# The down-projection of a SwiGLU layer by seven block products in place of eight

## The chip, the cores and the metric

One core of a Trainium2 chip runs the whole program. The metric is device microseconds of one execution; the kernel before took 1401.01 us, the median of 3 runs (1399.54 to 1403.0).

## The reference, cut to what matters

The program is a two-layer trunk over 512 rows of 1024 features (an attention mixer, a layer norm, a SwiGLU, a layer norm, a gated embedding, in each layer). The change touches the SwiGLU alone:

```python
def swiglu(x, w1, w3, w2):
    return (jax.nn.silu(x @ w1) * (x @ w3)) @ w2
...
x = layer_norm(DEEPNORM_ALPHA * x + swiglu(x, ffn_w1[i], ffn_w3[i], ffn_w2[i]), ln2_g[i], ln2_b[i])
```

The inner width is 2816, that is 22 tiles of 128 (the row tiles of w2). All data are float32. Each product is done in three TensorE passes on a high part rounded to fp32r and the remainder (high by low, high by high, low by high), which the helper `mm3` issues (L153 to L156).

## The kernel before

The rows of x lie in four SBUF tiles of 128 rows (`x[0]` to `x[3]`); their transposes, split into high and low parts, are `xTh` and `xTl`. `swiglu` walks over the 22 inner tiles in pairs. `up(f)` loads tile f of w1 and w3 in 512-column chunks of 256 KB through `wload` (L137: three `raw` buffers, a cast on ScalarE to the high part, a subtraction on VectorE or GpSimd, two to one, for the low part; four `hi` and four `lo` buffers of 128x1024). It makes two PSUM blocks of 24 matmuls each, then silu, the product of the two (L670), and the split of the result into high and low parts (`split`, L123 to L127), which are stationary operands of the down-projection.

`down(f0, gs)` loads two row tiles of w2 through the same `wload` and gives, for each of 4 row blocks and 2 column halves, 6 matmuls into one of two PSUM banks (`ps_pq`); VectorE adds each block to `x[t]` (L208 for the first pair, L212 after). So four inner tiles cost 16 PSUM blocks of 6, that is 96 matmuls. `down` of a pair is written after `up` of the next pair, and the last pair is done in `finish_rows` (L274), which adds the last blocks with their row sums and runs the layer norm of a row tile as soon as its two halves are there, then the transposes (`ps_xt`) and the first half of the gate (`ps_g`).

The order on each engine is not the written one: a scheduler orders the instructions ahead of time by written order as priority, by readiness of operands and by free buffers, with its own estimate of durations. On the chip each engine then runs its list in order. The pools that the change touches: `qk` (three buffers of 128x2048), `pl` (four of 128x1024), `pr` (two of 128x1536), `tmp` (four of 128x512), `g` (three of 128x2x512), `v` (eight of 128x1024), PSUM `ps_at` (4 banks), `ps_o` (2), `ps_pq` (2).

Of the kernel before, what the change touches and what calls it, by code (L numbers as in the profile page):

```python
# [8 lines left out]
F32 = mybir.dt.float32  # L9
F32R = mybir.dt.float32r  # L10
AF = mybir.ActivationFunctionType
ALU = mybir.AluOpType
AX = mybir.AxisListType

P = 128
LINE = 32
S = 512
NT = S // P
D = 1024
KT = D // P  # L20
DEPTH = 2
ALPHA = (2.0 * DEPTH) ** 0.25
# [18 lines left out]
QOFF = [0, 128, 384, 768]  # L41
WIDE = 1536
AHEAD = 0


@with_exitstack
def trunk(ctx: ExitStack, tc: tile.TileContext, a, out):
    nc = tc.nc

    def pool(name, bufs, **kw):  # L50
        return ctx.enter_context(tc.tile_pool(name=name, bufs=bufs, **kw))

    const = pool("const", 1)
    wpool = pool("w", 4)
    act = pool("act", 1)
# [3 lines left out]
    acts, dve, gps = nc.scalar, nc.vector, nc.gpsimd  # L59


    def temp(name, dtype=F32):
        return act.tile([P, S], dtype, tag="tmp", bufs=4, name=name)

    def wide(name, dtype=F32):
        return act.tile([P, WIDE], dtype, tag="pr", bufs=2, name=name)

    def spare(name, dtype=F32):
        return act.tile([P, D], dtype, tag="pl", bufs=4, name=name)

    def quad(name, dtype=F32R):
        return act.tile([P, 4, S], dtype, tag="qk", bufs=3, name=name)

    def row_tile(name, dtype=F32):
        return act.tile([P, D], dtype, tag="v", bufs=8, name=name)
# [4 lines left out]
    def bank(tag, bufs):  # L80
        return lambda name: psum.tile([P, S], F32, tag=tag, bufs=bufs, name=name)

    ps_at, ps_o, ps_pq = bank("at", 4), bank("o", 2), bank("pq", 2)
# [33 lines left out]

    xTh = const.tile([P, KT, S], F32R, name="xTh")
    xTl = const.tile([P, KT, S], F32R, name="xTl")
    x = [const.tile([P, D], F32, name=f"x{t}") for t in range(NT)]  # L120


    def split(hi, lo, src, scale=1.0, eng=None):  # L123

        if isinstance(scale, float) and scale == 1.0:
            nc.scalar.copy(hi, src)
            (eng or nc.vector).tensor_tensor(lo, src, hi.bitcast(F32), ALU.subtract)  # L127
        else:
            nc.scalar.mul(hi, src, scale)
            nc.vector.scalar_tensor_tensor(lo, src, scale, hi.bitcast(F32), ALU.mult, ALU.subtract)  # L130
# [8 lines left out]
    def wload(src, n, m):  # L139

        hi = wpool.tile([P, D], F32R, tag="hi", name="whi")
        lo = wpool.tile([P, D], F32R, tag="lo", name="wlo")
        for c in range(0, n * m, S):
            end = min(c + S, n * m)
            raw = wpool.tile([P, S], F32, tag="raw", bufs=3, name="wraw")[:, 0:end - c]
            nc.sync.dma_start(raw, src[:, c:end])
            count[0] += 1
            eng_hi, eng_lo = (v[count[0] % len(v)] for v in engines[0])
            (eng_hi.copy if eng_hi is acts else eng_hi.tensor_copy)(hi[:, c:end], raw)  # L149
            eng_lo.tensor_tensor(lo[:, c:end], raw, hi[:, c:end].bitcast(F32), ALU.subtract)  # L150
        return [t[:, 0:n * m].rearrange("p (n m) -> p n m", n=n) for t in (hi, lo)]

    def mm3(o, lhs, rhs, first, last):  # L153
        nc.tensor.matmul(o, lhsT=lhs[0], rhs=rhs[1], start=first, stop=False)  # L154
        nc.tensor.matmul(o, lhsT=lhs[0], rhs=rhs[0], start=False, stop=False)  # L155
        nc.tensor.matmul(o, lhsT=lhs[1], rhs=rhs[0], start=False, stop=last)  # L156

    def both(t, f):
        return (f(t[0]), f(t[1]))

    def row_piece(w, k):
        return wload(w[k * P:(k + 1) * P, :], 1, D)
# [3 lines left out]
    def blk(t):  # L166
        return slice(t * P, (t + 1) * P)
# [37 lines left out]
    def accumulate(t, half, ps, first, total=None):  # L205
        xs = x[t][:, half * S:(half + 1) * S]
        if first:
            nc.vector.scalar_tensor_tensor(xs, xs, ALPHA, ps, ALU.mult, ALU.add)  # L208
        elif total is not None:
            nc.vector.scalar_tensor_tensor(xs, xs, 1.0, ps, ALU.mult, ALU.add, accum_out=total)  # L210
        else:
            nc.vector.tensor_tensor(xs, xs, ps, ALU.add)  # L212

    def row_weights(w, rows):

        pieces = [row_piece(w, r) for r in rows]
        return lambda i, half: both(pieces[i], lambda v: v[:, 0, half * S:(half + 1) * S])

    def project_block(t, lhs, w, first, ps_of, sums=(None, None), halves=(0, 1)):

        n = len(lhs)
        for half in halves:
            ps = ps_of("ps_y")
            for i in range(n):
                mm3(ps, both(lhs[i], lambda v: v[:, blk(t)]), w(i, half), i == 0, i == n - 1)
            accumulate(t, half, ps, first, sums[half])
            yield 640 * n
# [32 lines left out]
    class Fill:  # L260
# [5 lines left out]
        def add(self, name, gen, after=()):  # L266
            self.items.append((name, gen, set(after)))

        def step(self):
            ready = [n for n, (_, _, after) in enumerate(self.items) if after <= self.done]  # L270
            if not ready:
                return None
            for n in ready[:1 + AHEAD]:
                name, gen, after = self.items[n]  # L274
# [350 lines left out]
    def gate(i, e, w, done):  # L625
        bg = broadcast(spare("bgate"), a["ple_b_gate"][i])
        pieces = [wload(w[0, c], 2, S) for c in range(4)]

        def block(t, half, cuts=1):
            ps = ps_at("ps_g")  # L630
            n = S // cuts
            for c in range(cuts):
                cs = slice(c * n, (c + 1) * n)
                hs = slice(half * S + c * n, half * S + (c + 1) * n)
                for k in range(KT):
                    mm3(ps[:, cs], x_block(k, t), both(pieces[k // 2], lambda v: v[:, k % 2, cs]), k == 0, k == KT - 1)
                s = temp("sg")[:, cs]
                nc.vector.tensor_tensor(s, ps[:, cs], bg[:, hs], ALU.add)
                nc.scalar.activation(s, s, AF.Sigmoid)
                nc.vector.tensor_tensor(s, s, e[t][:, hs], ALU.mult)  # L640
                nc.vector.tensor_tensor(x[t][:, hs], x[t][:, hs], s, ALU.add)
                if i == DEPTH - 1:
                    nc.sync.dma_start(out[0, blk(t), hs], x[t][:, hs])
            done(t, half)

        def rest():
            pieces[:] = [wload(w[1, c], 2, S) for c in range(4)]
            for t in range(NT):
                block(t, 1, 2 if i == DEPTH - 1 and t == NT - 1 else 1)

        return lambda t: block(t, 0), rest


    def swiglu(i, finish):
        w1, w3, w2 = a["ffn_w1"][i], a["ffn_w3"][i], a["ffn_w2"][i]
        nf = DFF // P

        def up(f, g, cuts=1):
            pieces = [wload(w[f], KT, P) for w in (w1, w3)]
            hps = [ps_at("ps_h") for _ in pieces]  # L660
            n = S // cuts
            for c in range(cuts):
                cs = slice(c * n, (c + 1) * n)
                for piece, ps in zip(pieces, hps):
                    for k in range(KT):
                        mm3(ps[:, cs], both(piece, lambda v: v[:, k, :]), both(xT, lambda v: v[:, k, cs]),
                            k == 0, k == KT - 1)
            s = temp("silu")
            nc.scalar.activation(s, hps[0], AF.Silu)
            nc.vector.tensor_tensor(s, s, hps[1], ALU.mult)  # L670
            split(g[0], g[1], s)

        def down(f0, gs):
            w = row_weights(w2, [f0 + j for j in range(len(gs))])
            for t in range(NT):
                for _ in project_block(t, gs, w, f0 == 0, ps_pq):
                    pass

        waiting = None
        for f in range(0, nf, 2):  # L680
            group = quad("gT")
            gs = [(group[:, 2 * j, :], group[:, 2 * j + 1, :]) for j in range(2)]
            for j in range(2):
                up(f + j, gs[j], 2 if f + j == 0 else 1)
            if waiting is not None:
                down(*waiting)
            waiting = (f, gs)
        f0, gs = waiting
        finish(gs, row_weights(w2, [f0 + j for j in range(len(gs))]))


    def mixer_mla_sb(norm, e):
# [293 lines left out]
    for i in range(DEPTH):  # L986
        def norm_params(gname, bname):
            return [broadcast(spare(n), a[n][i]) for n in (gname, bname)]
# [11 lines left out]
        def finish(gs, w):  # L1000
            first_half, rest = gate(i, e, a["w_gate"][i], done)
            finish_rows(gs, w, False, norm_params("ln2_g", "ln2_b"), after=first_half)
            rest()
# [105 lines left out]
```

## Time and profile before

| | |
|---|---|
| median of 3 runs | 1401.01 us (1399.54 to 1403.0) |
| profiled execution | 1401.66 us, span 1400.0 us |
| TensorE matmuls | 97% of the span busy |
| VectorE / ScalarE / GpSimd | 57% / 44% / 29% busy |
| mean granted TensorE clock | 0.993 of full speed |

The span is 40 slices of 35 us. The two SwiGLUs lie at about 303 to 652 us and at 985 to 1345 us. A busy TensorE is counted with modelled ends, so the distance between starts of matmuls says more than their durations. A VectorE instruction of the page overlaps the next one a little; the distance between starts is what it occupies.

### The profile page before, as it was taken

Reading aid. Unit: us, or ns where it says so; the run is one execution under the profiler, and the core shown is the slowest. Engines: PE = TensorE matmul, PEld = TensorE weight load, DVE = VectorE, ACT = ScalarE, POOL = GpSimd, SP = SyncE. Lnnn points to the kernel's source line nnn. Section 1 sums busy time; section 2 is a strip of 40 time slices with the busy share of each in tenths; the row PEclk is TensorE's granted clock in tenths of the full one; section 3 lists DMA queues with packets and bytes.
Section 4 is the critical chain, followed back from the end, with each engine's and each line's share of the span. In section 5 each row is a group of like instructions: output and inputs, shape, how many; then the busy total and the mean of one; then the engine's idle time right before and its main releaser. Section 6 shows DMA issues by size and latency. Waiting matters only on the chain.

```text
span 1400.0 us, 18875 instructions
## 1 busy us (share of the span) xinstructions
PE 1361.1 (97%) x6776; PEld 1139.6 (81%) x6776; DVE 797.0 (57%) x1492; ACT 611.6 (44%) x1269; POOL 408.8 (29%) x406
## 2 busy tenths in 40 slices
PE   8999999799999999999989999998999999999998
PEld 7888787588888888887879888876888888888877
DVE  4656778843444444448655775797434434444495
ACT  4656767552223222324456665754422223232252
POOL 5654733221111111112135454442211111111130
PEclk9999999999999999999999999999999999999999
DMA  6211312232322323332134222121423232322212
GB/s 232 94 40 42 125 60 73 78 117 80 106 91 91 105 94 107 102 102 78 62 107 137 91 91 69 64 88 68 136 76 104 94 105 100 110 91 98 98 61 98
DMA packets 69166, 131.75 MB, mean 94 GB/s; under 512 B 8128, under 2 KB 8896, under 8 KB 69056
## 3 DMA queue, kind: packets, MB, share of 16 engines
q1 hardware_dynamic: 66304, 120.75, 25.7%
q0 software_dynamic: 2768, 9.80, 2.1%
q8 instruction: 53, 0.87, 0.3%
q14 instruction: 41, 0.34, 0.1%
HBM read 127.80 MB, written 2.72 MB: 93 GB/s over the span
## 4 chain that ended last, share of the span: by engine, by line
PE 85%; DVE 7%; ACT 3%; DMA 3%; issue 2%; POOL 1%; SPq 0%; DVEq 0%; POOLq 0%; ACTq 0%
PE ps_h L154 11%; PE ps_h L155 11%; PE ps_h L156 11%; PE ps_y L154 7%; PE ps_y L155 7%; PE ps_y L156 7%; PE ps_qkT L154 2%; PE ps_qkT L155 2%; PE ps_qkT L156 2%; PE ps_o L408 2%; PE ps_g L154 2%; PE ps_g L156 2%; PE ps_g L155 2%; PE ps_z L545 1%; PE ps_t L440 1%
## 5 line engine op out<-in xcount | busy, mean ns | idle before, releaser
L150 POOL TENSOR_TENSOR wlo<-wraw,whi 128x512 fp32r<-128x512 f32 (+2 forms) x212 | 276.8, 1313 | 752.5 <-ACT whi L149 624.9
L149 ACT CAST whi<-wraw 128x512 fp32r<-128x512 f32 (+1 forms) x402 | 238.2, 616 | 553.8 <-PE ps_h L155 230.4
L154 PE MATMUL ps_h<-xTl,whi 128*128 128x512 f32 (+1 forms) x736 | 279.7, 380 | 0.0
L155 PE MATMUL ps_h<-xTh,whi 128*128 128x512 f32 (+1 forms) x736 | 279.5, 380 | 0.0
L156 PE MATMUL ps_h<-xTh,wlo 128*128 128x512 f32 (+1 forms) x736 | 279.3, 380 | 0.0
L150 DVE TENSOR_TENSOR wlo<-wraw,whi 128x512 fp32r<-128x512 f32 (+1 forms) x215 | 172.6, 816 | 133.3 <-ACT whi L149 132.4
L212 DVE TENSOR_TENSOR x<-x,ps_y 128x512 f32<-128x512 f32 x176 | 119.7, 682 | 145.8 <-PE ps_y L156 145.6
L156 PEld LDWEIGHTS ps_h<-xTh,wlo 128*128 128x128 f32 x736 | 138.2, 188 | 26.5
L155 PEld LDWEIGHTS ps_h<-xTh,whi 128*128 128x128 f32 x736 | 138.3, 188 | 26.3
L154 PEld LDWEIGHTS ps_h<-xTl,whi 128*128 128x128 f32 x736 | 138.4, 188 | 26.2
L155 PE MATMUL ps_y<-whi,gT 128*128 128x512 f32 x352 | 136.9, 389 | 0.0
L154 PE MATMUL ps_y<-wlo,gT 128*128 128x512 f32 x352 | 136.6, 390 | 0.0
L156 PE MATMUL ps_y<-whi,gT 128*128 128x512 f32 x352 | 136.1, 389 | 0.0
L670 DVE TENSOR_TENSOR silu<-silu,ps_h 128x512 f32<-128x512 f32 x44 | 30.3, 688 | 110.3 <-PE ps_h L156 108.4
L154 PE MATMUL ps_qkT<-xTl,whi 128*128 128x512 f32 x192 | 77.7, 405 | 1.7 <-ACT whi L149 0.9
L155 PEld LDWEIGHTS ps_y<-whi,gT 128*128 128x128 f32 x352 | 66.1, 188 | 13.7
L156 PEld LDWEIGHTS ps_y<-whi,gT 128*128 128x128 f32 x352 | 66.1, 188 | 13.7
L156 PE MATMUL ps_qkT<-xTh,wlo 128*128 128x512 f32 x192 | 77.2, 402 | 0.0
L154 PEld LDWEIGHTS ps_y<-wlo,gT 128*128 128x128 f32 x352 | 66.0, 188 | 13.6
L155 PE MATMUL ps_qkT<-xTh,whi 128*128 128x512 f32 x192 | 76.5, 399 | 0.0
L154 PE MATMUL ps_v<-wlo,xTh 128*128 128x256 f32 (+1 forms) x192 | 56.4, 294 | 6.6 <-DVE neg_tri L112 6.3
L155 PE MATMUL ps_v<-whi,xTh 128*128 128x256 f32 (+1 forms) x192 | 55.7, 291 | 0.0
(234 smaller groups left out, 2534.5 us busy)
## 6 DMA issues: line engine op xcount, KB each, us to landing
wraw<-in_ffn_w_dram SPq DMA_DIRECT2D x264, 256.0 KB, 2.7
wraw<-in_w_gate_dram SPq DMA_DIRECT2D x32, 256.0 KB, 2.8
wraw<-in_w_qkf_dram SPq DMA_DIRECT2D x32, 256.0 KB, 2.6
wraw<-in_w_qkb_dram SPq DMA_DIRECT2D x16, 256.0 KB, 2.8
wraw<-in_a_w_out_dram SPq DMA_DIRECT2D x16, 256.0 KB, 2.6
kbias<-nd_dram POOLq DMA_DIRECT2D x8, 512.0 KB, 5.0
wraw<-in_c_w_out_dram SPq DMA_DIRECT2D x16, 256.0 KB, 2.7
wraw<-in_w_vf_dram SPq DMA_DIRECT2D x15, 256.0 KB, 3.1
```

Source lines behind the costliest of these rows:

```text
L149: (eng_hi.copy if eng_hi is acts else eng_hi.tensor_copy)(hi[:, c:end], raw)
L150: eng_lo.tensor_tensor(lo[:, c:end], raw, hi[:, c:end].bitcast(F32), ALU.subtract)
L154: nc.tensor.matmul(o, lhsT=lhs[0], rhs=rhs[1], start=first, stop=False)
L155: nc.tensor.matmul(o, lhsT=lhs[0], rhs=rhs[0], start=False, stop=False)
L156: nc.tensor.matmul(o, lhsT=lhs[1], rhs=rhs[0], start=False, stop=last)
L212: nc.vector.tensor_tensor(xs, xs, ps, ALU.add)
L408: nc.tensor.matmul(o_ps[:, kb * P:], lhsT=val[:, c:c + 2 * HD], rhs=t, start=first and n == 0, stop=last and n == 1, skip_group_check=True)
L440: nc.tensor.transpose(u.ps[:, blk(qb - u.i)], u.h.pr[:, QOFF[qb] + u.i * P:QOFF[qb] + (u.i + 1) * P], ident)
L545: nc.tensor.matmul(u.z[:, c:u.n], lhsT=w, rhs=rhs, start=False, stop=i == len(mms) - 1, skip_group_check=True)
L670: nc.vector.tensor_tensor(s, s, hps[1], ALU.mult)
```

## The change

The inner tiles 0 to 19 are taken in five groups of four (the last pair, 20 and 21, stays as it was). The group's product, 512 rows by 512 inner columns by 1024 outputs, is cut in two along each dimension, and seven products of 256 x 256 x 512 are made from sums and differences of blocks in place of eight; each is 2 PSUM blocks of 6 matmuls (`ps_m`, in `ps_pq` and `ps_o`). The four inner tiles of a group are kept unsplit in float32 (`gb`, as blocks); the four row tiles of w2 come as two transfers of 1 MB into `w2raw`. `operands(m)` makes the sums of product m and splits both operands; it is written one product ahead. `down` is now a generator with one step for a product, and two steps are written behind each `up`; the last group's seven steps stand together, behind `up(20)`. Products 0, 5 and 6 are added to x at once, products 1 to 4 to running sums (`acc`, four tiles), which `flush()` adds to x, once in a layer, written between the last step and `up(21)`. `up(21)` stands directly ahead of `finish`.

```diff
--- before.py
+++ after.py
@@ -41,6 +41,7 @@
 QOFF = [0, 128, 384, 768]
 WIDE = 1536
 AHEAD = 0
+HALF = S // 2
 @with_exitstack
@@ -117,7 +118,8 @@
     xTh = const.tile([P, KT, S], F32R, name="xTh")
     xTl = const.tile([P, KT, S], F32R, name="xTl")
-    x = [const.tile([P, D], F32, name=f"x{t}") for t in range(NT)]
+    x_rows = const.tile([P, NT, D], F32, name="x")
+    x = [x_rows[:, t, :] for t in range(NT)]
     def split(hi, lo, src, scale=1.0, eng=None):
@@ -667,26 +669,137 @@
                             k == 0, k == KT - 1)
             s = temp("silu")
             nc.scalar.activation(s, hps[0], AF.Silu)
-            nc.vector.tensor_tensor(s, s, hps[1], ALU.mult)
-            split(g[0], g[1], s)
-        def down(f0, gs):
-            w = row_weights(w2, [f0 + j for j in range(len(gs))])
-            for t in range(NT):
-                for _ in project_block(t, gs, w, f0 == 0, ps_pq):
+            g(s, hps[1])
+        def as_parts(g):
+            def put(s, h):
+                nc.vector.tensor_tensor(s, s, h, ALU.mult)
+                split(g[0], g[1], s)
+            return put
+        def as_block(halves, p, k):
+            def put(s, h):
+                for n, half in enumerate(halves):
+                    fs = slice(n * HALF, (n + 1) * HALF)
+                    nc.vector.tensor_tensor(half[:, p, k, :], s[:, fs], h[:, fs], ALU.mult)
+            return put
+        sums = {}
+        def down(f0, halves):
+            first = f0 == 0
+            raw = []
+            for p in range(2):
+                t = quad("w2raw", F32)
+                nc.sync.dma_start(t.rearrange("p (k j) c -> p k (j c)", k=2),
+                                  w2[(f0 + 2 * p) * P:(f0 + 2 * p + 2) * P, :].rearrange("(k p) c -> p k c", k=2))
+                raw.append(t)
+            B = [[halves[i][:, :, k, :] for i in range(2)] for k in range(2)]
+            def W(j, k):
+                return [t[:, 2 * k + j, :] for t in raw]
+            s3, s1 = ([wide(n)[:, q * S:(q + 1) * S] for q in range(2)] for n in ("s3", "s1"))
+            n1, n2, n3, n4 = (temp(n).rearrange("p (q s) -> p q s", q=2) for n in ("n1", "n2", "n3", "n4"))
+            def add(o, a, b, eng):
+                for q in range(2):
+                    eng[q].tensor_tensor(o[q], a[q], b[q], ALU.add)
+            def operands(m):
+                tt = dve.tensor_tensor
+                ws, bs = [(W(0, 1), B[1][0]), (W(0, 0), B[0][0]), (s3, n3), (s1, n1), (s1, n2), (W(1, 1), n4),
+                          (s1, B[1][1])][m]
+                if m == 2:
+                    add(s3, W(0, 0), W(1, 0), (dve, gps))
+                    tt(n3, B[0][1], B[1][1], ALU.subtract)
+                elif m == 3:
+                    add(s1, W(1, 0), W(1, 1), (dve, gps))
+                    tt(n1, B[0][0], B[0][1], ALU.subtract)
+                elif m == 4:
+                    add(s1, s1, W(0, 0), (dve, gps))
+                    dve.scalar_tensor_tensor(n2, B[1][1], -1.0, n1, ALU.mult, ALU.subtract)
+                elif m == 5:
+                    tt(n4, n2, B[1][0], ALU.add)
+                elif m == 6:
+                    add(s1, s1, W(0, 1), (dve, gps))
+                parts = act.tile([P, 2, S], F32R, tag="g", bufs=3, name="bparts")
+                bh, bl = (parts[:, c, :].rearrange("p (q s) -> p q s", q=2) for c in range(2))
+                acts.copy(bh, bs)
+                dve.tensor_tensor(bl, bs, bh.bitcast(F32), ALU.subtract)
+                hi = wpool.tile([P, D], F32R, tag="hi", name="whi")
+                lo = wpool.tile([P, D], F32R, tag="lo", name="wlo")
+                wh, wl = ([v[:, q * S:(q + 1) * S] for q in range(2)] for v in (hi, lo))
+                for q in range(2):
+                    acts.copy(wh[q], ws[q])
+                    (dve, gps)[(q + m) % 2].tensor_tensor(wl[q], ws[q], wh[q].bitcast(F32), ALU.subtract)
+                return (bh, bl), (wh, wl)
+            ready = operands(0)
+            for m in range(7):
+                (bs, ws), ready = ready, operands(m + 1) if m < 6 else None
+                for tb in range(2):
+                    ps = (ps_pq, ps_o)[tb]("ps_m")
+                    for q in range(2):
+                        mm3(ps, both(bs, lambda v: v[:, q, blk(tb)]), both(ws, lambda v: v[q]), q == 0, q == 1)
+                    if m in (0, 5, 6):
+                        o = x[tb + 2 * (m == 6)][:, (m == 5) * S:(m == 5) * S + S]
+                        if first:
+                            dve.scalar_tensor_tensor(o, o, ALPHA, ps, ALU.mult, ALU.add)
+                        else:
+                            dve.tensor_tensor(o, o, ps, ALU.add)
+                    else:
+                        if first and tb == 0:
+                            sums[m] = row_tile("acc").rearrange("p (t c) -> p t c", t=2)
+                        o = sums[m][:, tb, :]
+                        if first:
+                            acts.copy(o, ps)
+                        else:
+                            dve.tensor_tensor(o, o, ps, ALU.add)
+                yield
+        def flush():
+            q1, q7, p5, p6 = (sums[m] for m in (1, 2, 3, 4))
+            h00, h01, h10, h11 = (x_rows[:, 2 * i:2 * i + 2, j * S:(j + 1) * S] for j in range(2) for i in range(2))
+            dve.tensor_tensor(p6, q1, p6, ALU.add)
+            gps.tensor_tensor(h00, h00, q1, ALU.add)
+            dve.tensor_tensor(h10, h10, q7, ALU.add)
+            dve.tensor_tensor(q7, q7, p5, ALU.subtract)
+            gps.tensor_tensor(h01, h01, p5, ALU.add)
+            dve.scalar_tensor_tensor(h11, h11, ALPHA, q7, ALU.mult, ALU.add)
+            dve.tensor_tensor(h10, h10, p6, ALU.subtract)
+            gps.tensor_tensor(h01, h01, p6, ALU.add)
+            dve.tensor_tensor(h11, h11, p6, ALU.subtract)
+        steps = iter(())
+        for f0 in range(0, nf - 2, 4):
+            halves = [spare("gb").rearrange("p (q k s) -> p q k s", q=2, k=2) for _ in range(2)]
+            for n in range(4):
+                up(f0 + n, as_block(halves, n // 2, n % 2), 2 if f0 + n == 0 else 1)
+                for _ in zip(range(2), steps):
                     pass
-        waiting = None
-        for f in range(0, nf, 2):
-            group = quad("gT")
-            gs = [(group[:, 2 * j, :], group[:, 2 * j + 1, :]) for j in range(2)]
-            for j in range(2):
-                up(f + j, gs[j], 2 if f + j == 0 else 1)
-            if waiting is not None:
-                down(*waiting)
-            waiting = (f, gs)
-        f0, gs = waiting
-        finish(gs, row_weights(w2, [f0 + j for j in range(len(gs))]))
+            for _ in steps:
+                pass
+            steps = down(f0, halves)
+        group = quad("gT")
+        gs = [(group[:, 2 * j, :], group[:, 2 * j + 1, :]) for j in range(2)]
+        up(nf - 2, as_parts(gs[0]))
+        for _ in steps:
+            pass
+        flush()
+        up(nf - 1, as_parts(gs[1]))
+        finish(gs, row_weights(w2, [nf - 2, nf - 1]))
     def mixer_mla_sb(norm, e):
```

## Rows read from the trace of the kernel before

**Rows 1.** The page's busy times: engine, busy us, share of the span, instructions.
```profile
PE 1361.1 (97%) x6776; PEld 1139.6 (81%) x6776; DVE 797.0 (57%) x1492; ACT 611.6 (44%) x1269; POOL 408.8 (29%) x406
```
**Rows 2.** Windows (start:end length, busy us and instructions by engine, clock, DMA): both SwiGLUs, their tails.
```profile
303.00:629.00 326.00, 326.00 (x1440) 269.96 (x1440) 142.44 (x194) 93.91 (x165) 55.06 (x41) 1.00 0.30 99
629.00:640.00 11.00, 11.00 (x50) 9.09 (x50) 4.94 (x8) 1.66 (x3) 0.00 (x0) 1.00 0.21 72
640.00:652.00 12.00, 12.00 (x59) 10.03 (x58) 11.45 (x21) 6.03 (x11) 4.79 (x7) 1.00 0.06 21
652.00:672.00 20.00, 19.08 (x92) 14.96 (x91) 18.48 (x32) 11.57 (x19) 6.58 (x8) 1.00 0.28 93
...
1345.00:1365.00 20.00, 18.42 (x90) 14.69 (x89) 19.40 (x31) 11.52 (x19) 6.61 (x8) 1.00 0.31 106
```
**Rows 3.** Timeline of TensorE, two blocks of the down-projection (start, duration, line, operation).
```profile
603.88 0.39 PE L154 MATMUL ps_y<-wlo,gT 128*128 128x512 f32 x1
...
606.37 0.39 PE L156 MATMUL ps_y<-whi,gT 128*128 128x512 f32 x1
```
**Rows 4.** Groups of the page: count, busy us and mean ns, then idle time before.
```profile
L155 PE MATMUL ps_y<-whi,gT 128*128 128x512 f32 x352 | 136.9, 389 | 0.0
```
**Rows 5.** Groups by shape on VectorE and GpSimd, the same columns.
```profile
L212 DVE TENSOR_TENSOR x<-x,ps_y 128x512 f32<-128x512 f32 x176 | 119.7, 682 | 145.8 <-PE ps_y L156 145.6
L197 DVE SCALAR_TENSOR_TENSOR ln<-x,neg_mean,ln_g 128x1024 f32<-128x1024 f32 x16 | 20.5, 1282 | 0.5
L127 DVE TENSOR_TENSOR val<-ps_v,val 128x256 fp32r<-128x256 f32 x24 | 9.8, 419 | 9.5 <-ACT val L126 9.4
L150 POOL TENSOR_TENSOR wlo<-wraw,whi 128x512 fp32r<-128x512 f32 x208 | 274.2, 1325 | 748.5 <-ACT whi L149 621.0 <-PE ps_y L156 85.3 <-DVE whi L149 12.7
```
**Rows 6.** Groups by shape of 345 to 625 us: the casts of weights on ScalarE.
```profile
L149 ACT CAST whi<-wraw 128x512 fp32r<-128x512 f32 x105 | 62.7, 620 | 208.0 <-PE ps_h L155 151.6 <-DMA wraw<-in_ffn_w_dram 30.3 <-PE ps_y L156 15.6
```
**Rows 7.** Timeline of VectorE: two equal subtractions, and the GpSimd instruction beside the second.
```profile
430.52 0.69 DVE L150 TENSOR_TENSOR wlo<-wraw,whi 128x512 fp32r<-128x512 f32 x1 [1.13 <-ACT whi L149]
...
445.25 1.30 POOL L150 TENSOR_TENSOR wlo<-wraw,whi 128x512 fp32r<-128x512 f32 x1 [12.08 <-ACT whi L149]
...
445.77 1.32 DVE L150 TENSOR_TENSOR wlo<-wraw,whi 128x512 fp32r<-128x512 f32 x1 [1.49 <-ACT whi L149]
```
**Rows 8.** Timeline of VectorE behind one `up`: starts of instructions back to back.
```profile
435.73 0.68 DVE L212 TENSOR_TENSOR x<-x,ps_y 128x512 f32<-128x512 f32 x1
436.33 0.68 DVE L127 TENSOR_TENSOR gT<-silu,gT 128x512 fp32r<-128x512 f32 x1
436.93 0.68 DVE L212 TENSOR_TENSOR x<-x,ps_y 128x512 f32<-128x512 f32 x1
```
**Rows 9.** Timeline of the first tail: layer norm of row tile 0, its transposes, the gate's start.
```profile
640.65 0.68 DVE L210 SCALAR_TENSOR_TENSOR x<-x,ps_y 128x512 f32<-128x512 f32 x1
641.37 0.21 DVE L195 TENSOR_SCALAR neg_mean<-sum,sum 128x1 f32<-128x1 f32 x1
...
648.53 1.03 PE L179 MATMUL ps_xt<-identr,x 128*128 128x128 f32 x8
...
652.14 0.39 PE L154 MATMUL ps_g<-wlo,xTh 128*128 128x512 f32 x1
```
**Rows 10.** Waits of TensorE over the whole span: for whom, us in total, times, longest.
```profile
PE ps_g L156 <- DVE xTl L127: 1.9, 3, 1.0
```
**Rows 11.** DMA issues: KB each, median us from issue to landing.
```profile
wraw<-in_ffn_w_dram SPq DMA_DIRECT2D x264, 256.0 KB, 2.7
x<-in_x_dram SPq DMA_DIRECT2D x4, 512.0 KB, 5.8
```

## The prediction

> **What bounds the kernel now.** I read the busy times first: TensorE is busy 97% of the span, VectorE 57%, ScalarE 44%, GpSimd 29% [rows 1]. An average hides stages, so next the windows: from 303 to 629 us, the body of the first SwiGLU, TensorE is busy 326.0 of 326.0 us while VectorE has 142.4 [rows 2]. The reader is to see that nothing but TensorE sets the time there, and that a matmul taken out shortens the span by its full distance. That distance is 326.0/1440 = 0.226 us; the timeline agrees, 12 matmuls start within 2.49 us, 2.49/11 = 0.226 us [rows 2, 3]. In the tails it is otherwise: from 640 to 652 us VectorE is busy 11.45 of 12, from 652 to 672 us 18.5 of 20, from 1345 to 1365 us 19.4 of 20, and TensorE loses 0.9 and 1.6 us in the last two [rows 2]. So the body is bound by TensorE and the tail, where the layer norm runs, nearly by VectorE. A gain in the body counts in full; what is late on VectorE when the body ends is paid in the tail.
>
> **The matmuls removed.** The down-projection has 352 matmuls of each of its three passes, 1056 [rows 4]. Four inner tiles cost 16 blocks of 6, that is 96; seven products of 2 blocks cost 84. Ten groups of four in two layers: 10 x 12 = 120 matmuls fewer, 120 x 0.2264 = 27.2 us. The shape of a matmul (128x128 stationary, 512 columns) and of the PSUM block stays, so the distance should stay. This is the only gain of size.
>
> **Elementwise work in the body, for a group of four inner tiles.** VectorE gives up 4 subtractions for gT, 2 of 16 block additions and its two thirds of 8 chunks of w2 (5.3); it takes on 7 subtractions for the low parts of the activations' sums, 7 for those of the weights' (the other 7 go to GpSimd), 4 half sums of weights (4 more on GpSimd) and 4 sums of activation blocks; 4 silu products become 8 of half the size (about 0.42 us each, by a 128x256 row [rows 5]). So some 40 instructions become 47 and 8 short ones. Before, a group was 288 matmuls, 65.2 us, and VectorE had 142.4/326.0 x 65.2 = 28.5 us in it [rows 2], 0.71 us each. After: 47 x 0.71 + 8 x 0.42 = 36.7 us in 276 x 0.2264 = 62.5 us, 59%. GpSimd: 5.3 + 7 + 4 = 16.3 instructions x 1.325 = 21.6 us [rows 5], 35%. ScalarE: 16 casts of w1 and w3, 21 casts of operands, 4 silus, 41 x 0.62 = 25.4 us [rows 6], 41%. All of it lies beside TensorE. What spoils it is that a subtraction of 0.69 us took 1.32 us where a GpSimd subtraction had begun 0.52 us before it [rows 7]. At worst every GpSimd instruction costs VectorE its own duration: 36.7 + 21.6 = 58 us, 93%, still below 62.5. So I cost the body at nothing. Its bounds: nothing below, because no matmul is waited for now; above, a wait at each product, the last rival below.
>
> What covers the operands in the body: two products stand together, 2 x 12 x 0.2264 = 5.4 us, then an `up` of 48 matmuls, 10.9 us. Of a product's operands the longest chain is one sum and three casts on ScalarE, then a subtraction on GpSimd, some 1.3 + 3 x 0.62 + 1.3 = 4.5 us from rows 5 to 7. It fits under the `up`; within a pair the second product's operands are to be there already. The four `hi` buffers, shared with w1 and w3, are the tight resource: casts of weights already sat 151.6 us waiting until TensorE released a buffer [rows 6], without a stall of TensorE. PSUM evictions have four banks for a pair's four blocks, one bank more than they need.
>
> **DMA.** The bytes stay. Per group 8 transfers of 256 KB become 2 of 1 MB. None of that size is in the trace; 256 KB land in 2.7 us, 512 KB in 5.8 [rows 11], so between 5.8 and 11.6 us for 1 MB, taken as 11, by the nearer row. SP issues in order, so chunks of w1 or w3 queued behind come later by as much; they are consumed 4 in 16.3 us with three buffers ahead. The raw tiles are wanted once a group, 62.5 us. Cost nothing; 0 to 3 us in all.
>
> **The last steps of a layer.** The last group's seven products stand together: 84 matmuls, 19.0 us, with no `up` between. The operands of three are ready (three `g` buffers), four are made in it. Then `up(21)`, 10.9 us, beside `flush`: six VectorE instructions of 1024 columns, 1.28 us by the layer norm's row [rows 5], and three on GpSimd. That shape is not in the trace on GpSimd; between 1.3 us (a 512-column one) and 2 x 1.3, and I take 2.6. Together 29.9 us of TensorE. VectorE in it: 14 evictions and 18.3 instructions between SBUF tiles (4 + 4 low parts, 2 weight sums, 2 block sums, 1 gT, 5.3 chunks of the last w1, w3 and w2) at 0.60 us from start to start [rows 8] = 19.4 us, and the flush with 6 x 1.2 = 7.2: 26.6 us, 89%. GpSimd: 8.7 x 1.3 + 7.8 = 19.1 us. By doubling wherever they meet, VectorE is behind by a few us. The scheduler can pull the first half of `up(21)` (24 matmuls, 5.4 us) between the steps, which hides much. I take 2 us for each layer, between 0 and 7.4 (the second rival).
>
> In this tail the row (0.69 us becoming 1.32 beside GpSimd [rows 7]) shows that the two engines hinder each other where both read SBUF twice. The Trainium skill ("SBUF — State Buffer", section "Who interferes with whom") has a stricter rule: a VectorE instruction with two SBUF inputs and a GpSimd instruction that reads SBUF exclude each other for the whole of the instruction. With it the tail is a sum over both engines, and the total goes from 1386 towards 1397; without it VectorE alone counts. The 1.32 us fits it (0.78 us left of the GpSimd instruction, and 0.6).
>
> **The layer norm's start.** Now the last 96 matmuls before the layer norm are `down(18, 19)` and the final pair mixed; row tile 0 has its second sum at 640.65 us and the last ps_y matmul stands right before 652.14, 11.5 us later; its transposes come at 648.53, 7.9 us behind the sum, and the gate starts as soon as ps_y ends [rows 9]. After the change only the final pair's 48 matmuls, 10.9 us, are left there: row tile 0 has its sums 2.7 + 0.6 us after their start, the transposes come 7.9 us later, at 11.2, past the end of ps_y at 10.9, and the splits follow with another 1 to 3 us. Each next row tile then follows at VectorE's pace, on which the flush may still lie. Four evictions that stood in this stretch are gone (2.4 us). I take 4 us for each layer, between 1 and 6. The activations of tile 21 (silu, product, cast, subtraction, about 2.6 us) are needed by the second half of each block; first halves of four blocks, 4 x 3 x 0.226 = 2.7 us, cover them, cost 0 (to 1).
>
> **The sum.** -27.2 + 2 x 2 + 2 x 4 = -15.2 us. On the profiled execution's own 1401.66 us (span 1400.0, the rest around it) that is 1386.5; the median shown is 0.65 us lower, so I forecast 1386 us.
>
> **The rivals.**
> (A) The gain is kept whole: the scheduler hides the last steps under `up(21)` and the layer norm finds other work for TensorE (the gate's blocks). 1401.0 - 27.2 = 1374 us, 1377 with small losses. For it: TensorE loses under 2 us in either tail now, and waits only 1.9 us for xTl in the whole span [rows 2, 10]. Against: VectorE there is above 90%.
> (B) VectorE and GpSimd together bound each tail. Instructions between SBUF tiles: 18.3 x 0.6 + 7.2 = 18.2 us on VectorE plus 19.1 on GpSimd, 37.3 against 29.9 us of TensorE: 7.4 us a layer in place of my 2. -27.2 + 2 x 7.4 + 2 x 4 = -4.4, 1397 us. For it: the 1.32 us of rows 7. Against: evictions can run beside GpSimd, the flush can run on behind.
> (C) Slower: the steps starve. If w1 and w3 hold the `hi` buffers (the 151.6 us of rows 6 show how they wait for release), a product's operands are made only when the previous product lets go; the chain of 4.5 us stands against 2.7 us of a product. 70 products: from 27.2/70 = 0.39 us of wait each the change loses. At 0.6 us, 42 us of waits: 1416 us. Against: only four of seven products have a product directly ahead of them in the body, and `up` gives 10.9 us to catch up.
>
> **How the numbers follow.** My forecast, 1380 to 1392 us, has 0.50. A has 0.17, B (1392 to 1400) 0.18, C 0.10, and 0.05 for waits in the steps that just eat the gain. The range for 8 in 10 leaves out C and the edges of A and B: 1375 to 1399 us. Less than 0.3% (4.2 us, about what a measurement of this kernel can tell from no change) is 1396.8 to 1405.2. Faster: forecast, A and over half of B, 0.78. Within: the rest of B and the 0.05, 0.12. Slower: 0.10.
>
> **What would show it.** Matmuls: 936 of the down-projection in place of 1056 (840 ps_m and 96 ps_y), at 0.226 us. Body: TensorE without gaps, VectorE near 60%, GpSimd near 35%. Tail: gaps or swapped order behind `up(20)` for each layer, and ps_g waiting for xTl or for xt of row tile 0. I am wrong if ps_m waits for wlo or bparts within the body (C), if the tail shows no gap (A), or if the distance of ps_m matmuls is over 0.23 us.

## The result, and the profile after

The changed kernel takes 1421.77 us (median of 4 runs, 1420.14 to 1423.98) against 1400.67 us for the kernel before (median of 4, one run more than at the start): a ratio of 1.0145, interval 1.013 to 1.0159. It is 21 us slower where I forecast 15 us faster.

First the body. These are windows of the changed kernel (columns as in rows 2) over the first SwiGLU; its first ps_h stands at 285.4 us, before at 284.6.

```profile
303.00:597.00 294.00, 294.00 (x1303) 243.70 (x1302) 179.54 (x232) 107.40 (x191) 96.40 (x71) 1.00 0.28 97
597.00:610.00 13.00, 8.19 (x28) 5.93 (x26) 9.88 (x9) 5.56 (x10) 8.17 (x6) 0.87 0.12 39
610.00:620.00 10.00, 6.78 (x28) 4.87 (x28) 10.00 (x13) 4.14 (x9) 6.39 (x4) 0.98 0.00 0
620.00:630.00 10.00, 10.00 (x38) 8.14 (x39) 8.04 (x10) 3.53 (x7) 6.34 (x5) 0.85 0.16 52
630.00:640.00 10.00, 10.00 (x46) 8.29 (x45) 10.00 (x11) 2.74 (x6) 2.35 (x2) 1.00 0.39 132
640.00:650.00 10.00, 3.92 (x17) 2.99 (x16) 10.00 (x7) 2.18 (x4) 8.25 (x3) 0.85 0.09 29
650.00:660.00 10.00, 9.38 (x33) 7.12 (x32) 5.93 (x14) 3.24 (x7) 1.27 (x3) 0.81 0.29 103
660.00:670.00 10.00, 6.56 (x31) 5.08 (x32) 9.96 (x15) 5.37 (x10) 5.49 (x8) 1.00 0.31 106
```

The reader is to see two kernels in one. To 597 us TensorE is busy 294.0 of 294.0 us, at 294.0/1303 = 0.226 us a matmul, the distance of rows 2 and 3. VectorE has 61% and GpSimd 33% there (59 and 35 forecast). Behind 597 us, where the last group's steps begin, TensorE idles 18.2 us in 73, where the whole tail before lost 0.9 us [rows 2]. The next stage (ps_v) began at 701.7 us before and begins at 714.2 now, by the groups of TensorE in 640 to 760 us (the first line is of the kernel before):

```profile
L154 PE MATMUL ps_v<-wlo,xTh x55: 277/285/370, 701.7 to 760.0; 128*128 128x272 f32 x32, 128*128 128x256 f32 x23
L156 PE MATMUL ps_v<-wlo,xTh x33: 278/288/371, 714.2 to 759.8; 128*128 128x272 f32 x32, 128*128 128x256 f32 x1
```

With 13.6 us of matmuls gone in the layer and a start 0.8 us later, the tail of one layer loses 12.5 - 0.8 + 13.6 = 25 us. The second layer does the same: its first ps_h is 11.5 us late (977.6 to 989.1) and the end 22.3 (1400.0 to 1422.3).

The waits of TensorE over the whole span (us in total, times, longest) name three places that were not there:

```profile
PE ps_y L156 <- DVE silu L677: 10.0, 2, 6.1
PE ps_m L156 <- DVE wlo L745: 8.9, 2, 4.4
...
PE ps_m L156 <- DVE acc L768: 6.6, 4, 3.0
```

Their number of times matters: 2, 2 and 4, so each is an event of the two tails (they stand behind 597 and behind 1300 us) and none of the body. The wait of ps_g for xTl rose from 1.9 us [rows 10] to 4.4.

**The gap at the last group's first product.** Timelines of SP, ScalarE and TensorE of the changed kernel, and the landing time of the two transfers issued at 581 us:

```profile
497.13 0.38 SPq L704 DMA_DIRECT2D w2raw<-in_ffn_w_dram  x1
...
580.96 0.94 SPq L704 DMA_DIRECT2D w2raw<-in_ffn_w_dram  x2
...
598.59 0.62 ACT L128 CAST gT<-silu 128x512 fp32r<-128x512 f32 x1 [5.06 <-DVE silu L677]
599.12 1.13 ACT L744 CAST whi<-w2raw 128x512 fp32r<-128x512 f32 x2
...
597.44 0.39 PE L158 MATMUL ps_h<-xTh,wlo 128*128 128x512 f32 x1
602.26 0.55 PE L156 MATMUL ps_m<-wlo,bparts 128*128 128x512 f32 x1 [4.43 <-DVE wlo L745]
...
DMA to landing us min/median/max: 7.8/7.8/7.8
```

Both 1 MB transfers of the last group are issued at 581 us, and the casts of its weights stand in ScalarE's list behind the cast for tile 20, which needs the end of `up(20)`. ScalarE, VectorE and GpSimd idle for 3 to 5 us ahead of that; nothing is busy, the work is in the wrong place. The data are not late on the chip: they land at 589 us, ten before the first cast (599.12 us). What TensorE waits for is the place of the casts in the list. Earlier groups had one of their two raw tiles loaded a group ahead: `w2raw` was issued in twos at 373 and 435 us, but at 497 us only once.

**The gap ahead of ps_y.** VectorE, GpSimd and TensorE, from 640 us:

```profile
640.10 3.30 POOL L779 TENSOR_TENSOR x<-x,acc 128x1024 f32<-128x1024 f32 x1 [2.96 <-PE ps_h L158]
641.08 2.88 DVE L152 TENSOR_TENSOR wlo<-wraw,whi 128x512 fp32r<-128x512 f32 x1
643.88 2.28 DVE L783 TENSOR_TENSOR x<-x,acc 128x1024 f32<-128x1024 f32 x1
645.04 3.31 POOL L782 TENSOR_TENSOR x<-x,acc 128x1024 f32<-128x1024 f32 x1
646.08 2.82 DVE L152 TENSOR_TENSOR wlo<-wraw,whi 128x512 fp32r<-128x512 f32 x1
648.83 0.67 DVE L677 TENSOR_TENSOR silu<-silu,ps_h 128x512 f32<-128x512 f32 x1
...
649.56 0.79 PE L156 MATMUL ps_y<-wlo,gT 128*128 128x512 f32 x1 [6.08 <-DVE silu L677]
```

A subtraction of 0.69 us takes 2.88 us: it begins at 641.08 and ends at 643.96, that is 0.56 us behind the end of the GpSimd addition at 643.40. The silu product that releases TensorE stands behind it in VectorE's list. The Trainium skill ("SBUF — State Buffer", section "Who interferes with whom") says that a VectorE instruction with two SBUF inputs and a GpSimd instruction that reads SBUF exclude each other for the whole instruction; this row is that rule, 2.3 us of waiting and 0.6 of work. The body has such clashes too: taking 0.69 us as the undisturbed duration, VectorE's instructions between SBUF tiles lose some 40 us by them from 303 to 597 us (an estimate from its timeline), and TensorE loses nothing. In the tail, from 597 to 650 us, they lose 17.

**Slow matmuls behind a gap.** TensorE, right after the 4.4 us gap:

```profile
603.47 0.63 PE L156 MATMUL ps_m<-wlo,bparts 128*128 128x512 f32 x1
603.89 0.63 PE L157 MATMUL ps_m<-whi,bparts 128*128 128x512 f32 x1
...
606.48 0.40 PE L158 MATMUL ps_m<-whi,bparts 128*128 128x512 f32 x1
606.72 0.39 PE L156 MATMUL ps_m<-wlo,bparts 128*128 128x512 f32 x1
```

The distance is 0.42 us and then 0.24: the lower of the two levels (1.2 GHz), then the upper (2.4). The granted clock is 0.55 from 602.2 to 606.0 us and 1.00 from there to 609.4 us. The windows above show it as 0.87, 0.85 and 0.81 of the clock; the second of these, behind waits of 1.8 and 1.3 us for evictions, has 38 matmuls in a full 10 us where 46 fit: 8/46 of 10 us, 1.7 us, lost without any idle time. Counted over the whole, some 25 matmuls in the first tail and 42 in the second are of this slow kind (over 0.5 us long in place of 0.39), and together they take 5.2 and 8.8 us more from start to start than at 0.226 us each. The kernel before has none in its two SwiGLUs and tails.

### The profile page after: what moved, and what is told of

Same layout as the page of the kernel before. It is cut to its first block, busy times and chain, and to the rows that moved or that the text cites. A ratio compares the mean times of both kernels' runs of the same rounds, so it can differ in the third digit from the quotient of the medians.

```text
span 1422.3 us, 18846 instructions
## 1 busy us (share of the span) xinstructions
PE 1351.7 (95%) x6656; PEld 1126.5 (79%) x6656; DVE 951.9 (67%) x1633; ACT 669.0 (47%) x1375; POOL 554.9 (39%) x497
## 4 chain that ended last, share of the span: by engine, by line
PE 80%; DVE 12%; ACT 2%; DMA 2%; issue 2%; POOL 1%; SPq 0%; DVEq 0%; POOLq 0%; ACTq 0%
PE ps_h L157 11%; PE ps_h L156 11%; PE ps_h L158 11%; PE ps_m L156 4%; PE ps_m L157 4%; PE ps_m L158 4%; PE ps_qkT L156 3%; PE ps_qkT L157 2%; PE ps_qkT L158 2%; PE ps_o L410 2%; PE ps_g L158 2%; PE ps_g L156 2%; PE ps_g L157 2%; PE ps_y L156 2%; DVE wlo L152 2%
## 5 line engine op out<-in xcount | busy, mean ns | idle before, releaser
L152 POOL TENSOR_TENSOR wlo<-wraw,whi 128x512 fp32r<-128x512 f32 (+3 forms) x187 | 244.6, 1316 | 415.0 <-ACT whi L151 353.9
L151 ACT CAST whi<-wraw 128x512 fp32r<-128x512 f32 (+1 forms) x322 | 190.4, 615 | 301.8 <-PE ps_h L157 75.3
L152 DVE TENSOR_TENSOR wlo<-wraw,whi 128x512 fp32r<-128x512 f32 x160 | 138.2, 875 | 84.9 <-ACT whi L151 81.6
L156 PE MATMUL ps_m<-wlo,bparts 128*128 128x512 f32 x280 | 112.8, 403 | 15.5 <-DVE wlo L745 8.9
L157 PE MATMUL ps_m<-whi,bparts 128*128 128x512 f32 x280 | 111.8, 399 | 0.0
L158 PE MATMUL ps_m<-whi,bparts 128*128 128x512 f32 x280 | 111.5, 398 | 0.0
L744 ACT CAST whi<-s 128x512 fp32r<-128x512 f32 x80 | 46.2, 619 | 120.9 <-PE ps_h L157 73.1
L745 POOL TENSOR_TENSOR wlo<-s,whi 128x512 fp32r<-128x512 f32 x40 | 53.2, 1333 | 98.2 <-ACT whi L744 98.2
L156 PEld LDWEIGHTS ps_m<-wlo,bparts 128*128 128x128 f32 x280 | 54.2, 194 | 29.6 <-DVE wlo L745 10.1
L745 POOL TENSOR_TENSOR wlo<-w2raw,whi 128x512 fp32r<-128x512 f32 x30 | 42.9, 1431 | 81.3 <-ACT whi L744 77.7
L158 PEld LDWEIGHTS ps_m<-whi,bparts 128*128 128x128 f32 x280 | 54.3, 194 | 11.7
```

What stands on the lines that cost most here:

```text
L744: acts.copy(wh[q], ws[q])
L745: (dve, gps)[(q + m) % 2].tensor_tensor(wl[q], ws[q], wh[q].bitcast(F32), ALU.subtract)
```

## The experiments

All versions start from the changed kernel unless it says otherwise; ratios are to the kernel before, run beside them.

| version | us | ratio, 95% interval |
|---|---|---|
| changed kernel | 1421.8 | 1.0145, 1.013 to 1.0159 |
| four groups | 1393.1 | 0.9944, 0.9924 to 0.9963 |
| no flush | 1400.2 | 0.9992, 0.998 to 1.0004 |
| no GpSimd in the tail | 1403.1 | 1.0013, 1.0 to 1.0025 |
| steps spread 4 and 3 | 1418.8 | 1.0123, 1.0102 to 1.0145 |
| gT elsewhere | 1401.4 | 0.9998, 0.9989 to 1.0008 |
| flush on VectorE | 1408.9 | 1.0062, 1.0042 to 1.0082 |
| operands on VectorE | 1415.9 | 1.0105, 1.0071 to 1.0138 |
| four groups, gT elsewhere | 1378.0 | 0.9834, 0.982 to 0.9849 |
| gT elsewhere, no GpSimd | 1389.9 | 0.9914, 0.9898 to 0.993 |
| gT elsewhere, no GpSimd, spread | 1396.5 | 0.9963, 0.9951 to 0.9974 |
| gT elsewhere, no GpSimd, no flush | 1387.8 | 0.99, 0.9873 to 0.9928 |

**Four groups in place of five.** Three plain pairs end the layer, as before.

```diff
-        for f0 in range(0, nf - 2, 4):
+        cut = nf - 6
+        for f0 in range(0, cut, 4):
...
+        for f in range(cut, nf, 2):
...
+                up(f + j, as_parts(gs[j]))
+                for _ in zip(range(2), steps):
+                    pass
+            if f == cut + 2:
+                for _ in steps:
+                    pass
+                flush()
+            if waiting is not None:
+                plain(*waiting)
```

The last group's steps stand two behind each `up` here, as in the body; so both their density and what follows them change.

> Only inner tiles 0 to 15 (four groups) by seven products; 16 to 21 in plain pairs as before, the last group's steps two behind each up, flush behind the fourth of them. Where the loss is: the changed kernel keeps TensorE full in the body, and loses some 25 us in each layer behind up(20). If that place (the steps standing together, and the flush ahead of tile 21's silu) is the cause, the tail is the old one again and the gain is 2 x 4 x 12 matmuls x 0.2264 = 21.7 us: 1379 to 1384 us. If the flush or the products cost the same wherever they stand (rival), some 10 us a layer stay lost: about 1400.

1393.1 us: between the two forecasts. The old tail is back (ps_y waits for no silu), but one wait of the changed kernel stands unmoved to the digit, now at 539 us, in the middle of the layer, where nothing is short:

```profile
PE ps_m L156 <- DVE wlo L745: 8.9, 2, 4.4
...
539.29 0.50 PE L156 MATMUL ps_m<-wlo,bparts 128*128 128x512 f32 x1 [4.43 <-DVE wlo L745]
...
519.11 0.94 SPq L704 DMA_DIRECT2D w2raw<-in_ffn_w_dram  x2
```

It belongs to "the last group", not to the tail: again both transfers are issued together, 20 us ahead of the product, and again the casts stand behind the cast for the tile of the `up` before (536 us), though the data had landed by 529. What is new at the last group is gT: it takes one of the three `qk` buffers just ahead of the group, and the group's two raw tiles must both wait for those of the group before. That gave theory W (the late w2 transfers; late in the order, not on the chip).

**No flush.**

```diff
-        flush()
```

> The changed kernel without flush (products 1 to 4 are made but their sums are not added to x). Theory F (the flush, standing ahead of silu's product of tile 21 in VectorE's list, is the main price): the 6.1 us gap and the slow clock behind it go in both layers, about 10 us each, 1400 us. Theory S (seven steps together are too dense) and theory P (VectorE and GpSimd exclude each other over the whole tail): the gaps at ps_m stay, under 8 us each layer come back, 1406 to 1416.

1400.2 us, 21.6 less: what F forecast. In this version x lacks the sums of products 1 to 4. It doesn't part the flush's own work from its GpSimd additions; the next ones do.

**No GpSimd in the tail.**

```diff
-        def down(f0, halves):
+        def down(f0, halves, gps=gps):
...
-            steps = down(f0, halves)
+            steps = down(f0, halves, dve if f0 + 4 == nf - 2 else gps)
... (in flush)
-            gps.tensor_tensor(h00, h00, q1, ALU.add)
+            dve.tensor_tensor(h00, h00, q1, ALU.add)
...
```

The other two GpSimd additions of the flush change in the same way.

> In the last group's operands and in the flush, GpSimd's instructions go to VectorE (the body keeps GpSimd). VectorE then has some 34 us of work at 0.6 us each in 29.9 us of TensorE. Theory P (two instructions that read SBUF twice wait for each other, 1.7 us in place of 0.6): VectorE's instructions fall back to 0.6 to 0.7 us, the tail loses 5 to 8 us a layer in place of 25, about 1385 to 1395 us. Theory S (load and chain of the seven steps, whichever engine): VectorE has more to do, no better than 1420.

1403.1 us: VectorE got more work and the kernel 18.6 us faster. That speaks for P and against S; the size was 8 us short of P's range with the gap of W still there:

```profile
PE ps_m L156 <- DVE wlo L745: 8.3, 4, 3.4
```

**Steps spread.**

```diff
+        for _ in zip(range(4), steps):
+            pass
+        up(nf - 1, as_parts(gs[1]))
         for _ in steps:
             pass
         flush()
-        up(nf - 1, as_parts(gs[1]))
```

> The same instructions; the last group's steps are written four behind up(20) and three behind up(21), and the flush behind them, so that silu of tile 21 stands ahead of the flush. Theory S: TensorE has up(21) to cover the chains, most comes back, about 1390 to 1397. Theory P: the same pair of engines has the same 37 us of work between up(20) and the layer norm, the loss moves to the layer norm's start; 1405 to 1420.

1418.8 us, P's range. The wait moved from silu to the layer norm's start (`ps_xt`, and `ps_y` for the row sums' evictions). S falls.

```profile
PE ps_xt L181 <- DVE x L203: 9.0, 4, 3.4
...
PE ps_y L156 <- DVE x L212: 8.6, 3, 4.7
```

**gT in another pool.**

```diff
-        group = quad("gT")
-        gs = [(group[:, 2 * j, :], group[:, 2 * j + 1, :]) for j in range(2)]
+        gs = [tuple(act.tile([P, S], F32R, tag="pT", bufs=7, name="gT") for _ in range(2)) for _ in range(2)]
```

> The changed kernel with gT of the last pair in four 128x512 buffers of another pool (pT, idle there), so that w2raw has the three qk buffers to itself. In the changed kernel gT takes one of the three, the last group's two 1 MB transfers are both issued at 581 us and the operands of its first product come 4.4 us late (in the first version with four groups the same 4.4 us stand at its last group). Theory W (late w2 transfers open the first gap): the 4.4 us and the slow clock behind it go in both layers, 1408 to 1413 us. If the first gap is elementwise load: no change, 1420 or more.

1401.4 us, 20.4 less, more than W forecast. SP and ScalarE of this version:

```profile
495.76 0.89 SPq L704 DMA_DIRECT2D w2raw<-in_ffn_w_dram  x2
...
557.91 0.38 SPq L704 DMA_DIRECT2D w2raw<-in_ffn_w_dram  x1
...
582.72 1.14 ACT L744 CAST whi<-w2raw 128x512 fp32r<-128x512 f32 x2 [3.85 <-issue]
```

The last group's first raw tile is issued at 496 us, the second at 558 in place of 581, and the casts stand at 583 in place of 599. No instruction was taken away. The gap of 4.4 us is gone, its slow matmuls too, and the operands' work has left the crowded stretch: in all, TensorE idles 15 us less in the two layers, and 6 us less go to matmuls at the lower level. A wait of 2.9 us in the steps is there instead (610.8 us), with the cause of P in it: the addition for `s` takes 2.84 us beside an addition of the flush on GpSimd, and the cast that releases TensorE needs it.

```profile
606.75 2.80 POOL L776 TENSOR_TENSOR x<-x,acc 128x1024 f32<-128x1024 f32 x1
607.26 2.84 DVE L717 TENSOR_TENSOR s<-s,w2raw 128x512 f32<-128x512 f32 x1
```

**Flush on VectorE, and operands on VectorE, each by itself.** The edits are the two halves of "no GpSimd in the tail".

> Only the flush's three GpSimd additions go to VectorE; operands as in the changed kernel. Theory P, with the flush as its place (3.3 us additions on GpSimd hold VectorE's list, silu's product of tile 21 behind it): the 6 us gap ahead of ps_y shrinks below 2 us, 1402 to 1410. Theory F (the flush's own work on VectorE, 7.2 us and now 10.8, is the price): no better, 1420 to 1428.

> Only the last group's operands are made without GpSimd; the flush keeps its three additions there. Theory P with its place in the steps: gaps at ps_m shrink, 1405 to 1412; if the flush is the place: 1416 or more. With the run before it parts the 18.6 us that leaving out both gave.

1408.9 us, 12.8 less, and 1415.9 us, 5.9 less; together 18.7, as both had given (18.6). So some two thirds of P lie in three additions of the flush. F falls as the main price: the flush with more work on VectorE is cheaper, and 8.8 of the 21.6 us that leaving it out gave remain. The second scatters widely (1410.8 to 1421.2) and lies between its two forecasts, so its 5.9 us is rough. Nor does it tell the exclusion from GpSimd's longer duration in a product's chain (1.29 us for a 128x512 subtraction, 0.69 on VectorE): no version parts these two.

**Four groups, and gT of tiles 16 and 17 elsewhere.** The edits of the first and of the fifth version together.

> Four groups as in the first version, with gT of tiles 16 and 17 in the pT buffers. Theory W: the 4.4 us gap at the last group's first product and its slow clock go in both layers, 1393 less 9 to 12: 1380 to 1384 us, the whole gain of 96 matmuls. Otherwise 1393.

1378.0 us, 15 less than with four groups alone, a little more than W forecast, and better than both kernels. The stretch around the last group, and the layer norm's start, as windows; and the flush's last addition on GpSimd:

```profile
550.00:590.00 40.00, 40.00 (x178) 33.14 (x177) 32.44 (x40) 14.93 (x27) 13.63 (x10) 1.00 0.33 112
590.00:600.00 10.00, 10.00 (x46) 8.29 (x45) 3.38 (x6) 1.64 (x3) 2.96 (x2) 1.00 0.24 80
...
640.00:650.00 10.00, 9.38 (x42) 7.43 (x40) 9.32 (x17) 5.14 (x10) 3.53 (x5) 1.00 0.48 158
650.00:660.00 10.00, 9.63 (x48) 7.95 (x49) 9.86 (x15) 5.81 (x9) 2.87 (x4) 1.00 0.17 54
...
590.57 2.40 POOL L782 TENSOR_TENSOR x<-x,acc 128x1024 f32<-128x1024 f32 x1
```

VectorE is busy 81% in the first, with its part of the flush in it, and TensorE misses nothing: the same products and the same flush, GpSimd and all, are free where `up` stands beside them. 96 matmuls x 0.2264 = 21.7 us were to come, 23.9 did (interval 21.2 to 25.2). No matmul of its two SwiGLUs and tails runs at the lower level.

**Both repairs on five groups.**

> Five groups, gT in the pT buffers, and no GpSimd in the last group's operands and in the flush. If theories W (-20.4 us by itself) and P (-18.6 us by itself) name two separate causes, they add up: 1421.8 - 39 = 1383 us. If they are one gap seen twice (the late weights pushed everything onto GpSimd's and VectorE's busiest stretch), little more than W alone: 1395 to 1400.

The edits of "gT in another pool" and "no GpSimd in the tail" together. 1389.9 us, between the two forecasts: 11.5 less than gT alone, not 18.6. W and P are two causes that overlap by some 7 us. In the steps VectorE now runs at its own pace, 0.60 us from start to start, and TensorE has two gaps under 0.4 us in them; behind them it still waits 1.9 us for silu of tile 21, at the end of the flush in VectorE's list:

```profile
601.76 0.68 DVE L745 TENSOR_TENSOR wlo<-s,whi 128x512 fp32r<-128x512 f32 x1
602.36 0.68 DVE L768 TENSOR_TENSOR acc<-acc,ps_m 128x512 f32<-128x512 f32 x1
602.96 0.68 DVE L745 TENSOR_TENSOR wlo<-s,whi 128x512 fp32r<-128x512 f32 x1
```

**The same, spread.**

> As the run before it, with the last group's steps written four behind up(20) and three behind up(21), and the flush behind them. Theory S (the steps stand too densely): 5 us less than the run before, 1378 to 1381. If VectorE's amount of work sets the tail, the flush lands on the layer norm: as the run before or up to 6 us more.

1396.5 us, 6.6 more, just beyond the second forecast, with the layer norm's transposes waiting 14.7 us in all:

```profile
PE ps_xt L181 <- DVE x L203: 14.7, 4, 6.7
```

S falls again: spreading the steps gains nothing, and the flush directly ahead of the layer norm is worse.

**Both repairs, without the flush** (x lacks the sums of products 1 to 4).

> Five groups, gT in pT, no GpSimd in the last operands, and no flush at all (the sums of products 1 to 4 are not added to x). The version with the flush on VectorE took 1389.9 us, some 16 us above the whole gain of 27.2 us. If the layer norm's start is what is left (only 48 matmuls stand beside it, 4 us a layer in the prediction), 8 us or more stay: 1382 to 1386. If the flush on VectorE is what is left: 1374 to 1378.

1387.8 us (1382.5 to 1390.6), 2 us above the nearer forecast: 2 us less than with the flush, within its own scatter. The flush, once it is on VectorE, is nearly free, and the layer norm's start is what is left. Windows of this version:

```profile
620.00:630.00 10.00, 10.00 (x46) 8.29 (x45) 4.96 (x7) 4.12 (x8) 2.59 (x2) 1.00 0.37 133
630.00:640.00 10.00, 8.71 (x39) 6.88 (x37) 6.74 (x14) 3.98 (x8) 1.95 (x3) 1.00 0.23 79
640.00:650.00 10.00, 7.23 (x35) 5.62 (x36) 9.96 (x19) 4.95 (x10) 5.20 (x8) 1.00 0.31 106
650.00:660.00 10.00, 6.45 (x21) 4.72 (x20) 7.14 (x11) 4.76 (x8) 3.03 (x4) 0.68 0.00 0
```

From 630 to 660 us TensorE idles 7.6 us and ends at 0.68 of its clock, with VectorE at half load just before. All of it is waiting of `ps_xt` and `ps_g`, so nothing is left over from the steps; the row tiles' layer norms come too late for the 48 matmuls that stand beside them. With a plain pair's matmuls mixed in, as in the four groups with gT elsewhere, TensorE loses 1.0 us from 640 to 660 us (windows above), where that version has the same work. The second layer of this version loses less there, 3.7 us.

## Why the prediction was wrong

**The matmuls removed: right.** 120 fewer at an unchanged distance; the version with four groups gained all of its 96.

**Elementwise work in the body: right.** VectorE at 61%, no wait of ps_m in the body. Rival C (starving steps) did not occur: 70 products, waits in the two tails only. So it is luck for C that the kernel came out slower, as C alone had it. My signs of A and of C did not come, and a distance over 0.23 us came only behind gaps; none of the signs looked at how long the tail's gaps are.

**The DMA step failed.** I wrote "Cost nothing; 0 to 3 us in all", from bytes and from the duration of a transfer. The transfer was shorter than I took it (6.0 us in the median against 11), and still its place cost 20.4 us (13.3 us when GpSimd is out of the tail). The step prices the transfers and never asks who else takes a `qk` buffer: gT does, directly ahead of the last group. With it, the operands of the last group, which I had as "ready" for three products when its steps begin, were not begun; their data lay there from 589 us on, but the scheduler had put their casts behind the end of `up(20)`. Why it put them there no run shows. That it puts them earlier when gT is elsewhere is shown by the version with gT in another pool (583 us), and in four groups the same change takes the wait away.

**The last steps: the mechanism right, the size wrong.** I took 2 us a layer and put 7.4 us a layer (rival B) at 0.18. Taking GpSimd out of the tail gave 18.6 us for two layers, 11.5 with the transfers mended: 6 to 9 us a layer. That is rival B in size, by the exclusion that the row of 1.32 us [rows 7] already showed in small. What I missed in it is where it strikes: not as a sum over both engines (the body carries more of it for nothing), but as single GpSimd additions that hold up the VectorE instructions standing ahead of one on which TensorE waits. Such an addition takes 2.4 us where VectorE does not hinder it (I had taken 2.6), and 2.7 to 3.3 in the two tails of the changed kernel. So the silu product of tile 21, which I had costed at 0 to 1 us, became the longest gap, 6.1 us.

**The layer norm's start: right, in kind and size.** 4 us a layer forecast (1 to 6). TensorE's waits of `ps_xt` and `ps_g` there are 4.9 and 4.0 us in the two tails of the changed kernel, 0.8 and 1.6 before. For the first tail:

```profile
PE ps_xt L181 <- DVE x L203: 2.2, 1, 2.2
PE ps_g L158 <- DVE xTl L129: 2.2, 2, 1.6
PE ps_g L156 <- ACT xTh L128: 0.5, 2, 0.2
```

With both other causes mended and no flush it is what is left: 1387.8 us is 14 us above the whole gain, 1401.0 - 27.2 = 1373.8, with waits there of 7.6 and 3.7 us.

**The clock: a term that my sum does not have.** I wrote that the shape of a matmul stays, "so the distance should stay". It stayed in the body; behind several gaps of the tails it was 0.42 us. That costs 14 us in the changed kernel, 3 in the version with both repairs, and nothing in the four groups with gT elsewhere, whose longest gap there is 1.0 us.

**The sum.** By the repairs: 1401.0 - 27.2 + 20.4 (transfers) + 11.5 (GpSimd in the tail) + 16.1 (what is left over) = 1421.8 us. The order of the repairs decides how the overlap of 7 us is shared, and each term holds the slow matmuls behind its gaps. By the traces: the changed kernel lies 22.3 + 27.2 = 49.5 us above the whole gain. In the two layers from the first ps_h on, TensorE idles 34.9 us, 2.9 before: 8.9 ahead of the last group's first product, 6.6 for evictions between the steps, 10.0 for silu of tile 21, 8.9 at the layer norm's start (2.4 before), 0.5 as before. With the 14 us of slow matmuls that is 46 of the 49.5 us. My terms for it were 4 us for the last steps and nothing for the transfers (25.5 us together), 8 for the layer norm (6.5 more than before), and none for the clock (14).

What stays open: the some 3.5 us that neither count holds, and how the gain from the operands without GpSimd is shared between the exclusion and GpSimd's longer durations.

## What to carry to other kernels

When a loop's last turn is followed by something else, go through its pools once more: the consumer behind it may take the buffer that let the loads run ahead. Where a matmul count is cut at the price of elementwise work, put the reduced form where other matmuls stand beside it and leave the end of the stage plain: with gT elsewhere, four groups with the old tail beat five groups by 12 us, though the five had GpSimd out of the tail as well and save 24 matmuls more. And look at which instruction stands behind a long GpSimd addition in VectorE's list, not at the engines' busy shares. Price a gap of TensorE with the slow matmuls behind it: here they cost 14 us beside 32 of added idle time.

## What the hardware showed that I had not expected

A VectorE subtraction of 0.69 us took up to 2.88 us beside a 3.3 us GpSimd addition, and ended 0.56 us after it. The 1024-column GpSimd addition took 2.40 us beside VectorE instructions with one input in PSUM, and 2.7 to 3.3 us in the two tails of the changed kernel, where a VectorE instruction with two inputs in SBUF was under way as it began. After the idle gap of 4.4 us nine matmuls of TensorE came 0.42 us apart before they returned to 0.23 us (602.26 to 606.02 us), so that gap cost 1.7 us more than its own length (9 x 0.42 - 9 x 0.226). A 1 MB transfer landed in 6.0 us in the median, where 512 KB had taken 5.8 [rows 11].
